# Moving the operands of TensorE's products to other byte offsets in SBUF: a conditioned decoder layer on one core

## The chip, the cores and the metric

The kernel runs on one core of one Trainium2 chip. The metric is the device time of one execution in microseconds (us), as the median of several runs. In the text, TensorE is PE (its weight loads PEld), VectorE is DVE, ScalarE is ACT, GpSimd is POOL and SyncE is SP, which issues most DMAs. SBUF is the on-chip memory of 128 partitions; a tile's "start" is its first byte within each partition. PSUM takes the results of TensorE.

## The reference

One layer of a decoder trunk for a batch of 1, 256 tokens, width 2048, in float32, followed by an RMS norm:

```python
mods = (silu(c) @ ada_w + ada_b).reshape(b, 9, d)
h = modulate(x, ffn1_norm, mods[:, 0], mods[:, 1])
x = x + 0.5 * mods[:, 2] * swiglu(h, ffn1_w_gate, ffn1_w_up, ffn1_w_down)   # 2048 -> 5632 -> 2048
h = modulate(x, mix_norm, mods[:, 3], mods[:, 4])
proj = h @ w_in                                       # columns for both mixers and the two gates
y_a = gated_delta_net(...) @ gdn_w_up                 # 8 heads of 128
y_b = sparse_attention(...) @ nsa_w_up                # 8 heads of 128
y = (m_a * y_a + m_b * y_b) @ w_out
x = x + mods[:, 5] * y
h = modulate(x, ffn2_norm, mods[:, 6], mods[:, 7])
x = x + 0.5 * mods[:, 8] * swiglu(h, ffn2_w_gate, ffn2_w_up, ffn2_w_down)
return rms_norm(x, final_norm)
```

Nearly all of the arithmetic lies in the products with the large weight matrices, which are read from HBM once.

## The kernel before, in words

Activations are kept transposed: a tile has 128 of the 2048 channels on its partitions and the 256 tokens along the free dimension. Weights arrive from HBM as tiles "raw" of 128 partitions by 8 slices of 128 columns (512 KB each), issued by SP.

To reach float32 accuracy with TensorE's fast float32r format, both operands of a product are split into a high and a low part. ACT copies raw to whi (line 186, or 357), which rounds it, and DVE writes the remainder raw - whi to wlo (line 187, or 358). Activations are pairs of 128 x 2 x 256: high part, then low part; they are called hpair (the input of a stage), apair (SwiGLU's result), xa (the unmodulated input of the second feed-forward stage), and oA, Vt, aT, Z, WT (the two mixers' outputs, which take over buffers of these names). The function product (line 192) issues, for each of its slices of 128 channels, two matmuls: line 196 with whi stationary and both halves of the pair moving (512 columns), then line 198 with wlo stationary and the high half moving (256 columns). This is called a pair of matmuls in the text; its weight loads are separate instructions on PEld, one for each matmul. The function block_rows (line 353) does the same in three matmuls of 256 columns for each slice (line 363); it serves the first stage's gate and up products and the first products of the stages that follow.

Order of the work: the start and the first feed-forward stage (functions start and ffn), the projections W_in with the two mixers beside them, the merge (line 1099: for each of 16 output tiles one weight tile of 16 slices; the first product takes slices 0 to 7 with the eight oA, the second slices 8 to 15 with Vt, aT, Z, WT, twice), W_out, the second feed-forward stage and the final norm. The reductions for the modulation (line 248, DVE) are spread between the products.

Memory: tiles come from pools, and a pool takes the next free stretch of SBUF when it is opened; within a pool, tiles stand in the order of their first use, each rounded up to 32 bytes. So a tile's start is the sum of all sizes before it. consts holds cf, vec (629 floats), cm (160 bytes), cr, cact and modc (9 x 16 floats); wp holds raw (8 buffers of 4096 bytes), whi and wlo (3 each); tp holds scratch tiles; nrm small tiles of the norms; hp the 16 hpair. The pool mp of the mixers is opened where the first stage's buffers were, so its tiles wait until these are done; its small tiles (gnw, na, ss, sk, m2 and so on, 4 to 480 bytes) stand between the large ones and set the starts of those behind them. A framework schedules the instructions of each engine from their dependences and the order of the code.

Of the kernel before, what the change touches and what calls it, by code (L numbers as in the profile page):

```python
# [18 lines left out]
F32 = mybir.dt.float32  # L19
F32R = mybir.dt.float32r  # L20
I32 = mybir.dt.int32
U8 = mybir.dt.uint8
# [5 lines left out]
P = 128  # L28
S = 256
D = 2048  # L30
KT = D // P
# [11 lines left out]
SIZES = ((4,), (4,), (4,), (4,))  # L43
LAG = 3
RES = 4
LT = 0
NE = 2
GK = 4
# [6 lines left out]
NB = 15  # L55
# [49 lines left out]
def trunk(tc, a, out, stage=99, dbg=None):  # L105
    nc = tc.nc
    ctx = ExitStack()
    with ctx:
        consts = ctx.enter_context(tc.tile_pool(name="consts", bufs=1))
# [13 lines left out]

        cf = consts.tile([P, C_END], F32, name="cf")
        nc.sync.dma_start(cf[:, :C_TRI], a["consts"][:, :C_TRI])
        vec = consts.tile([P, sum(n for _, n in VEC)], F32, name="vec")
        cm = consts.tile([P, 160], U8, name="cm")
        cr = consts.tile([P, 3, P], F32R, name="cr")
        ident = cf[:, C_ID:C_ID + P]
        ones = cf[:, C_ONE:C_ONE + P]  # L130
# [99 lines left out]
            nc.vector.tensor_sub(pair[:, 1], x, pair[:, 0])  # L230


        modc = consts.tile([P, 9, KT], F32, name="modc")
        ada_q = []

        def ada_cols(m, d, now=False):
# [47 lines left out]


        nrm = ctx.enter_context(tc.tile_pool(name="nrm", bufs=1))

        def square(ssq, d):
            if d == 0:
# [256 lines left out]
        def paces(*spans):  # L546
            todo = [(n, pace(total, n)) for total, n in spans]

            def f():
                while todo and todo[0][0] == 0:  # L550
                    todo.pop(0)
                if not todo:
                    return 0
                todo[0] = (todo[0][0] - 1, todo[0][1])
                return todo[0][1]()
            return f
# [29 lines left out]
        xpool.close()  # L586
        with ExitStack() as mx:
            mp = mx.enter_context(tc.tile_pool(name="mp", bufs=1))
            tk = paces((4, 31 - 2 * NE), (20, 20), (24, 36))

            beside = []
# [20 lines left out]
                return big(tag, BIG[tag], (P, 2, S), F32R)  # L612

            oA, oB = [None] * H, [None] * H
            gnw = mp.tile([P, 1], F32, name="gnw")
            nc.vector.tensor_scalar(gnw, V["gnw"], 0.5, None, op0=OP.mult)


# [1 line left out]
            both(win(0), sm)  # L620
            tok = mp.tile([P, 2, P], F32, name="tok")
            ge = mp.tile([P, 2, 2, 8], F32, name="ge")
            ngc = mp.tile([P, 2, 8], F32, name="ngc")
            na = mp.tile([P, 1], F32, name="na")
            beta = tok[:, :, 0:8]
            gtok = tok[:, :, 32:40]
            gate = tok[:, :, 64:88]
# [53 lines left out]
                return o  # L681

            def small(tag):
                return mp.tile([P, 4], F32, tag=tag, name=tag, bufs=2)

            def s3(t):
                return t.rearrange("p (a b) -> p a b", a=2)
# [17 lines left out]
            def gdn_group(h0, q, k, v):  # L705
# [3 lines left out]
                def tsl(p):  # L709
                    return slice(p * P, (p + 1) * P)  # L710

                ss = mp.tile([P, 2, 4], F32, tag="ss", name="ss", bufs=2)

                def flip(src):
                    pt = ptile((P, 4, P))
# [15 lines left out]
                pt = flip(q)  # L731
                squares(pt, ss[:, 1])
                nc.vector.tensor_scalar(ss, ss, 4 * EPS, None, op0=OP.add)
                rs = rsqrt(mp, ss, "rs")
                sk = small("sk")
                nc.vector.scalar_tensor_tensor(sk, rs[:, 0], 0.5 * RS, ss[:, 0], op0=OP.mult, op1=OP.mult)
                Cc = small("Cc")
# [136 lines left out]
                nc.vector.scalar_tensor_tensor(r2, rq, 1.0 / HD, rq, op0=OP.mult, op1=OP.mult)  # L874
                nc.vector.tensor_mul(so, so, r2)
                nc.vector.tensor_scalar(so, so, EPS, None, op0=OP.add)
                ro = rsqrt(mp, so, "ro")
                nc.vector.scalar_tensor_tensor(ro, ro, RS, rq, op0=OP.mult, op1=OP.mult)
                nc.vector.tensor_mul(o, o, ro.unsqueeze(2).to_broadcast([P, 4, P]))
                pt = ptile((P, 4, P))  # L880
# [18 lines left out]

            kcmp = mp.tile([P, 2 * NB], F32, name="kcmp")
            vcmp = mp.tile([16, 2, P], F32, name="vcmp")

            def compress():
                for b in range(2):
                    cat = mp.tile([P, 2, S], F32, tag="kk", name="cat", bufs=2)
                    for g in range(2):
                        both(win(W_KV + 2 * b + g, False), cat[:, g])
                        yield  # L910
                    G = mp.tile([P, 32, 32], F32, tag="G", name="G", bufs=1)
                    nc.gpsimd.memset(G[:, :, 2 * NB:], 0.0)
                    for g in range(2):
                        src = cat[:, g]
                        blocks = bass.AP(tensor=src.tensor, offset=src.offset, ap=[list(src.ap[0]), [1, 32], [16, NB]])
                        nc.vector.tensor_add(G[:, :, g * NB:(g + 1) * NB], blocks,
                                             V["pos"][:, 32 * b:32 * b + 32].unsqueeze(2).to_broadcast([P, 32, NB]))
                    ph = ftile()
                    for r in range(4):
                        (raw, _), = wload(a["cw1"][b][:, 8 * r:8 * r + 8], 8)  # L920
                        for j in range(8):
                            jj = 8 * r + j
                            q = slice(32 * (j % 4), 32 * (j % 4) + 32)
                            nc.tensor.matmul(ph[q, :P], G[:, jj], raw[:, j], start=(jj < 4), stop=(jj >= 28),
                                             skip_group_check=True)
                        yield
                    hs = mp.tile([P, P], F32, tag="hs", name="hs", bufs=1)
                    nc.scalar.activation(hs, ph[:, :P], AF.Copy)
                    pt = ftile()
                    nc.tensor.matmul(pt[:, :2 * NB], hs, cf[:, C_I32:C_I32 + 2 * NB], start=True, stop=True)  # L930
                    hid = mp.tile([P, 2 * NB], F32, tag="hid", name="hid", bufs=1)
                    nc.scalar.activation(hid, pt[:, :2 * NB], AF.Identity, bias=V["b1"][:, b:b + 1])
                    th = tmpc()[:, :2 * NB]
                    nc.scalar.activation(th, hid, AF.Tanh, scale=0.5)
                    hT2 = tmpc()[:, :2 * NB]
                    nc.vector.scalar_tensor_tensor(hT2, th, 1.0, hid, op0=OP.add, op1=OP.mult)
                    w2 = V["w2"][:, b * P:(b + 1) * P]
                    pc = ftile()
                    if b == 0:
                        nc.tensor.matmul(pc[:, :2 * NB], w2, hT2, start=True, stop=True)  # L940
                        nc.scalar.activation(kcmp, pc[:, :2 * NB], AF.Copy, scale=0.5)
                    else:
                        for g in range(2):
# [42 lines left out]
            def compressed(g, qs, gg):  # L986

                psc = ptile((P, 2, 4, 16))
                for qt in range(2):
                    for r in range(4):  # L990
                        nc.tensor.matmul(psc[:, qt, r, :NB], qs[r][:, qt * P:(qt + 1) * P],
                                         kcmp[:, g * NB:(g + 1) * NB], start=True, stop=True)
                sc = mp.tile([P, 2, 4, NB], F32, tag="sc", name="sc", bufs=1)
                cmask = cf[:, C_CMP:C_CMP + 32].rearrange("p (a b) -> p a b", a=2)
                for qt in range(2):
                    nc.vector.tensor_add(sc[:, qt], psc[:, qt, :, :NB],
                                         cmask[:, qt, :NB].unsqueeze(1).to_broadcast([P, 4, NB]))
                cmx = mp.tile([P, 8], F32, tag="cmx", name="cmx", bufs=2)
                scf = sc.rearrange("p a b c -> p (a b) c")
                nc.vector.tensor_reduce(cmx, scf, axis=AX.X, op=OP.max)  # L1000
                nc.vector.tensor_scalar(cmx, cmx, NEG / 10, None, op0=OP.max)
                nc.vector.tensor_sub(scf, scf, cmx.unsqueeze(2).to_broadcast([P, 8, NB]))
                nc.scalar.activation(sc, sc, AF.Exp, scale=SCALE)
                den = mp.tile([P, 8], F32, tag="den", name="den", bufs=2)
                nc.vector.tensor_reduce(den, scf, axis=AX.X, op=OP.add)
                nc.vector.tensor_scalar(den, den, 0.5, None, op0=OP.max)
                nc.vector.reciprocal(den, den)
                d3 = den.rearrange("p (q r) -> p q r", q=2)
                nc.vector.tensor_mul(d3, d3, gg[:, :, :, 0])
                nc.vector.tensor_mul(scf, scf, den.unsqueeze(2).to_broadcast([P, 8, NB]))  # L1010
                return sc

            def attend(g, kk, vt, qs):
# [3 lines left out]
                def soft(r, qt):  # L1017
# [4 lines left out]
                    for b in range(2):  # L1022
# [1 line left out]
                                         start=(b == 0), stop=False, skip_group_check=True)  # L1024
                    nc.tensor.matmul(ps[:, :, n - P:n], ident_r, cr[:, 2].unsqueeze(1).to_broadcast([P, 2, P]),
                                     start=False, stop=True, skip_group_check=True)
                    m2 = mp.tile([P, 2], F32, tag="m2", name="m2", bufs=4)
                    nc.vector.tensor_reduce(m2, ps[:, :, :n], axis=AX.X, op=OP.max)
                    nc.vector.tensor_scalar(m2, m2, -SCALE, None, op0=OP.mult)
                    p_ = pr[r, qt] = big(*PR[(2 * r + qt) % 3], (P, 2, S))  # L1030
                    dn = mp.tile([P, 2], F32, tag="dn", name="dn", bufs=4)
                    for b in range(2):
                        nc.scalar.activation(p_[:, b, :n], ps[:, b, :n], AF.Exp, bias=m2[:, b:b + 1],
                                             scale=SCALE, accum_out=dn[:, b:b + 1])
# [189 lines left out]
```

## Time and profile before

| | us |
|---|---|
| median of 3 runs (lowest, highest) | 2324.71 (2324.65, 2325.98) |
| the profiled execution | 2323.47 |
| its span, first to last instruction | 2321.6 |
| busy: PE, PEld, DVE, ACT | 2272.6, 2028.3, 1776.4, 1133.3 |

The mean granted TensorE clock of the profiled execution was 0.997 of full speed. 564 MB were read from HBM, 245 GB/s over the span. How to read the views: the page lists the busy time of each engine and the chain of work that ended last, followed back from the end; the groups put together instructions of one line, operation and shape, with their count, total busy time and mean duration, and after the bar the idle time ahead of them and what ended it; the timeline lists instructions by start time. Matmuls are pipelined, so a matmul's duration in the profile is longer than the distance from its start to the next one's.

### The profile page before, as it was taken

To read this page: it belongs to the slowest core of one execution; us is meant where nothing else is said; L and a number is where in the kernel's file an instruction comes from. 1 tells how busy PE (TensorE), PEld (TensorE's weight loads), DVE (VectorE), ACT (ScalarE), POOL (GpSimd) and SP (SyncE) were. 2 spreads that over 40 slices of the span, in tenths; PEclk is the share of its full clock that TensorE was granted. 3 is DMA by queue.
4 is the path that set the end of the run, shared out by engine and by line. 5 is a ranking of instruction groups with operands and counts; after the bars stand their busy time and mean duration, and the time that the engine had idled before them with its cause. 6 is when DMAs were issued, how large, how long until landed. Compare 5 with 4: busy or idle time off the path is not lost.

```text
span 2321.6 us, 39012 instructions
## 1 busy us (share of the span) xinstructions
PE 2272.6 (98%) x15130; PEld 2028.3 (87%) x15130; DVE 1776.4 (77%) x2896; ACT 1133.3 (49%) x1788; POOL 1.5 (0%) x8
## 2 busy tenths in 40 slices
PE   6999999999999999999999999999999999999997
PEld 5999988888888978887888888889888888888886
DVE  6799888878887787789997887787666666555565
ACT  3544554434444565554555445556444444344453
POOL 0000000000000000000000000000000000000000
PEclk9999999999999999999999999999999999999999
DMA  8999689888987646548677897665777777665663
GB/s 317 318 331 332 200 280 335 296 297 322 337 308 248 213 141 199 185 156 268 238 270 244 312 318 262 221 229 183 244 244 243 238 235 216 192 198 190 183 189 104
DMA packets 174493, 571.00 MB, mean 246 GB/s; under 512 B 17890, under 2 KB 18146, under 8 KB 174308
## 3 DMA queue, kind: packets, MB, share of 16 engines
q1 hardware_dynamic: 173584, 566.09, 73.0%
q8 instruction: 118, 1.93, 0.3%
q10 hardware_dynamic: 724, 2.43, 0.3%
q14 instruction: 67, 0.55, 0.1%
HBM read 564.25 MB, written 4.19 MB: 245 GB/s over the span
## 4 chain that ended last, share of the span: by engine, by line
PE 90%; DVE 6%; ACT 2%; DMA 1%; issue 1%; DVEq 0%; SPq 0%; ACTq 0%
PE mm L196 48%; PE mm L198 26%; PE mm L363 9%; PE c L363 2%; DVE adaraw L248 1%; DVE wlo L187 1%; DVE wlo L358 1%; DMA raw<-in_win_dram 1%; PE c L433 1%; DMA cf<-in_consts_dram 0%; PE c L1023 0%; ACT whi L186 0%; ACT junk L723 0%; PE c L800 0%; DMA raw<-in_w1gu_dram 0%
## 5 line engine op out<-in xcount | busy, mean ns | idle before, releaser
L196 PE MATMUL mm<-hpair,whi 128*128 128x512 f32 x3536 | 1237.7, 392 | 2.0 <-ACT t L218 2.0
L187 DVE TENSOR_TENSOR wlo<-raw,whi 128x1024 fp32r<-128x1024 f32 (+1 forms) x666 | 796.8, 1196 | 419.3 <-ACT whi L186 417.2
L186 ACT ACTIVATE whi<-raw 128x1024 fp32r<-128x1024 f32 (+1 forms) x666 | 691.9, 1039 | 755.1 <-PE mm L196 381.7
L198 PE MATMUL mm<-hpair,wlo 128*128 128x256 f32 x3536 | 1002.7, 284 | 2.6 <-DVE wlo L187 2.6
L196 PEld LDWEIGHTS mm<-hpair,whi 128*128 128x128 f32 x3536 | 664.4, 188 | 140.6 <-ACT t L218 2.5
L198 PEld LDWEIGHTS mm<-hpair,wlo 128*128 128x128 f32 x3536 | 668.7, 189 | 6.5 <-DVE wlo L187 4.0
L196 PE MATMUL mm<-apair,whi 128*128 128x512 f32 x1408 | 488.3, 390 | 0.0
L198 PE MATMUL mm<-apair,wlo 128*128 128x256 f32 x1408 | 397.1, 282 | 0.0
L196 PEld LDWEIGHTS mm<-apair,whi 128*128 128x128 f32 x1408 | 264.4, 188 | 55.4
L363 PE MATMUL mm<-hpair,whi 128*128 128x256 f32 x1472 | 260.7, 280 | 5.7 <-ACT whi L357 5.7
L198 PEld LDWEIGHTS mm<-apair,wlo 128*128 128x128 f32 x1408 | 266.1, 189 | 0.0
L363 PEld LDWEIGHTS mm<-hpair,whi 128*128 128x128 f32 x1472 | 225.9, 189 | 6.0 <-ACT whi L357 6.0
L363 PE MATMUL mm<-hpair,wlo 128*128 128x256 f32 x736 | 207.2, 282 | 3.1 <-DVE wlo L358 3.0
L248 DVE CUSTOM_DVE_ANT_0 adaraw<-adaraw,cact,vec 128x1024 f32<-128x1024 f32 x144 | 183.6, 1275 | 13.2 <-DMA adaraw<-in_ada_w_dram 13.2
L248 DVE CUSTOM_DVE_ANT_0 adaraw<-adaraw,cact,part 128x1024 f32<-128x1024 f32 x144 | 183.8, 1277 | 0.0
L357 ACT ACTIVATE whi<-raw 128x1024 fp32r<-128x1024 f32 x112 | 118.3, 1058 | 113.6 <-PE mm L363 44.3
L358 DVE TENSOR_TENSOR wlo<-raw,whi 128x1024 fp32r<-128x1024 f32 x112 | 136.1, 1220 | 34.0 <-ACT whi L357 33.5
L363 PEld LDWEIGHTS mm<-hpair,wlo 128*128 128x128 f32 x736 | 139.2, 189 | 4.2 <-DVE wlo L358 3.8
L222 ACT ACTIVATE t<-mm 128x256 f32<-128x256 f32 x237 | 86.5, 367 | 2.6 <-PE mm L198 2.6
L225 DVE TENSOR_TENSOR t<-mm,t 128x256 f32<-128x256 f32 x193 | 80.5, 417 | 2.7 <-ACT t L222 2.5
L530 DVE SCALAR_TENSOR_TENSOR xT<-mm,g,xT 128x256 f32<-128x256 f32 x128 | 61.5, 481 | 7.1 <-PE mm L198 5.4
L515 ACT ACTIVATE t<-t 128x256 f32<-128x256 f32 x63 | 25.9, 411 | 50.1 <-DVE t L225 50.1
(359 smaller groups left out, 1502.3 us busy)
## 6 DMA issues: line engine op xcount, KB each, us to landing
adaraw<-in_ada_w_dram SPq DMA_DIRECT2D x288, 512.0 KB, 5.7
raw<-in_w2gu_dram SPq DMA_DIRECT2D x180, 512.0 KB, 4.6
raw<-in_w1gu_dram SPq DMA_DIRECT2D x176, 512.0 KB, 5.9
raw<-in_win_dram SPq DMA_DIRECT2D x158, 512.0 KB, 5.2
raw<-in_w1d_dram SPq DMA_DIRECT2D x64, 512.0 KB, 5.1
raw<-in_w2d_dram SPq DMA_DIRECT2D x64, 512.0 KB, 4.1
raw<-in_wup_dram SPq DMA_DIRECT2D x32, 512.0 KB, 4.9
raw<-in_wout_dram SPq DMA_DIRECT2D x32, 512.0 KB, 4.7
```

The costliest lines, as they stand in the source:

```text
L186: nc.scalar.activation(hi[:, :n], raw[:, :n], AF.Copy)
L187: behind(nc.vector.tensor_sub(lo[:, :n], raw[:, :n], hi[:, :n]))
L196: nc.tensor.matmul(ps[:, :], hi, pairs[k][:, :, :].rearrange("p a b -> p (a b)"), start=(k == 0), stop=False, skip_group_check=True)
L198: nc.tensor.matmul(ps[:, S:2 * S], lo, pairs[k][:, 0, :], start=False, stop=(k == n - 1), skip_group_check=True)
L222: nc.scalar.activation(t, ps[:, S:2 * S], AF.Copy)
L225: nc.vector.tensor_add(o, ps[:, :S], t)
L248: nc.vector.tensor_tensor_reduce(out=raw, in0=raw, in1=cact[:, hf * HC:(hf + 1) * HC], scale=1.0, scalar=part[0], op0=OP.mult, op1=OP.add, ...
L357: nc.scalar.activation(hi, raw, AF.Copy)
L358: behind(nc.vector.tensor_sub(lo, raw, hi))
L363: nc.tensor.matmul(ps[:, w], l[:, w, k], h[:, r], start=(first and w == k == x == 0), stop=(last and k == kb - 1 and x == 2), skip_group_c ...
L515: nc.scalar.activation(s, g, AF.Silu, bias=bg)
L530: nc.vector.scalar_tensor_tensor(xT[:, d], pd[:, j * S:(j + 1) * S], g05[:, d:d + 1], xT[:, d], op0=OP.mult, op1=OP.add)
```

## The change

No instruction is added to the computation or taken from it, and no size of an operation changes. The change moves tiles to other starts:

- consts: vec is rounded up to 640 floats, cm to 256 bytes, modc to 10 x 16 floats, so that all that follows starts at multiples of 128.
- nrm gets a tile "pad" of 40 floats that nothing uses; it shifts hp and everything behind it.
- The mixers' small tiles move from mp to a pool of their own, ms, which is opened behind mp.

```diff
+PAD = 40
...
-        vec = consts.tile([P, sum(n for _, n in VEC)], F32, name="vec")
-        cm = consts.tile([P, 160], U8, name="cm")
+        nv = sum(n for _, n in VEC)
+        vec = consts.tile([P, -(-nv // 32) * 32], F32, name="vec")[:, :nv]
+        cm = consts.tile([P, 256], U8, name="cm")[:, :160]
...
-        modc = consts.tile([P, 9, KT], F32, name="modc")
+        modc = consts.tile([P, 10, KT], F32, name="modc")[:, :9]
...
         nrm = ctx.enter_context(tc.tile_pool(name="nrm", bufs=1))
+        nrm.tile([P, PAD], F32, name="pad")
...
             mp = mx.enter_context(tc.tile_pool(name="mp", bufs=1))
+            ms = mx.enter_context(tc.tile_pool(name="ms", bufs=1))
...
-            gnw = mp.tile([P, 1], F32, name="gnw")
+            gnw = ms.tile([P, 1], F32, name="gnw")
...
-            na = mp.tile([P, 1], F32, name="na")
+            na = ms.tile([P, 1], F32, name="na")
```

and so on for ngc, ss, the tiles of small(), rsqrt's, kcmp, hid, sc, cmx, den, m2 and dn. The starts in the two built programs, in bytes from the partition's beginning (of the first buffer; all buffers of a tile have the same remainder modulo 128):

| tile | role in a product | start before | modulo 128 | start after | modulo 128 |
|---|---|---|---|---|---|
| raw | what whi and wlo are split from | 35392 | 64 | 35584 | 0 |
| whi | stationary | 68160 | 64 | 68352 | 0 |
| wlo | stationary | 80448 | 64 | 80640 | 0 |
| hpair | moving | 102496 | 96 | 102848 | 64 |
| apair, xa | moving | 151648 | 96 | 152000 | 64 |
| Vt, aT, Z, WT | moving | 166752, 170848, 148832, 175968 | 96 | 166464, 170560, 149056, 175680 | 64 |
| oA | moving | 197408 | 32 | 196672 | 64 |

Slices of whi and wlo lie 512 bytes apart, the two halves of a pair 1024, so they have the same remainders.

The schedule changes at a few places, because the tiles of ms lie in memory that nothing used before them. On ACT, near the program's start, before (cact is the activated conditioning vector, t the squares of the input, cr constants for the mixers, rb the inverse norms spread over the partitions):

```order
L148 ACTIVATE cact<-c 128x512
L431 ACTIVATE t<-xT 128x256 x15
L156 ACTIVATE cr<-cf 128x128
L483 ACTIVATE rb<-c 128x256
L323 ACTIVATE hpair<-t,modc 128x256 x2
L357 ACTIVATE whi<-raw 128x1024
```

The same place after; na is the exponential of one parameter vector of the delta-rule mixer:

```order
L151 ACTIVATE cact<-c 128x512
L435 ACTIVATE t<-xT 128x256 x15
L159 ACTIVATE cr<-cf 128x128
L645 ACT_TABLE_LOAD
L645 ACTIVATE na<-vec 8x1
L487 ACTIVATE rb<-c 128x256
L327 ACTIVATE hpair<-t,modc 128x256 x2
L361 ACTIVATE whi<-raw 128x1024
```

The exponential and a load of its table moved here from the mixers' beginning. The second place on ACT is the end of the function start, where the first SwiGLU activations (t from gu) and the splits of their results (apair) begin; before:

```order
L323 ACTIVATE hpair<-t,modc 128x256
L357 ACTIVATE whi<-raw 128x1024 x4
L470 ACTIVATE t<-gu 128x256
L229 ACTIVATE apair<-t 128x256
L357 ACTIVATE whi<-raw 128x1024
L470 ACTIVATE t<-gu 128x256
```

and after:

```order
L327 ACTIVATE hpair<-t,modc 128x256
L361 ACTIVATE whi<-raw 128x1024 x4
L474 ACT_TABLE_LOAD
L474 ACTIVATE t<-gu 128x256
L361 ACTIVATE whi<-raw 128x1024
L232 ACTIVATE apair<-t 128x256
```

A second table load stands here, and the split of the result stands behind the next copy of weights. In all, ACT has seven table loads after and five before. On DVE, the one-column operation for gnw moves from the mixers' beginning to the program's start; TensorE's order changes in one place, where two small transposes stand two matmuls later.

More of the change, by code (lines that the diff above doesn't have):

```diff
@@ L622, in trunk @@
             ge = mp.tile([P, 2, 2, 8], F32, name="ge")
-            ngc = mp.tile([P, 2, 8], F32, name="ngc")
-            na = mp.tile([P, 1], F32, name="na")
+            ngc = ms.tile([P, 2, 8], F32, name="ngc")
+            na = ms.tile([P, 1], F32, name="na")
             beta = tok[:, :, 0:8]
@@ L683, in small @@
             def small(tag):
-                return mp.tile([P, 4], F32, tag=tag, name=tag, bufs=2)
+                return ms.tile([P, 4], F32, tag=tag, name=tag, bufs=2)
             def s3(t):
@@ L710, in tsl @@
                     return slice(p * P, (p + 1) * P)
-                ss = mp.tile([P, 2, 4], F32, tag="ss", name="ss", bufs=2)
+                ss = ms.tile([P, 2, 4], F32, tag="ss", name="ss", bufs=2)
                 def flip(src):
@@ L733, in gdn_group @@
                 nc.vector.tensor_scalar(ss, ss, 4 * EPS, None, op0=OP.add)
-                rs = rsqrt(mp, ss, "rs")
+                rs = rsqrt(ms, ss, "rs")
                 sk = small("sk")
@@ L876, in gdn_group @@
                 nc.vector.tensor_scalar(so, so, EPS, None, op0=OP.add)
-                ro = rsqrt(mp, so, "ro")
+                ro = rsqrt(ms, so, "ro")
                 nc.vector.scalar_tensor_tensor(ro, ro, RS, rq, op0=OP.mult, op1=OP.mult)
@@ L898, in gdn_out @@
                     split(oA[h], sg)
-            kcmp = mp.tile([P, 2 * NB], F32, name="kcmp")
+            kcmp = ms.tile([P, 2 * NB], F32, name="kcmp")
             vcmp = mp.tile([16, 2, P], F32, name="vcmp")
@@ L930, in compress @@
                     nc.tensor.matmul(pt[:, :2 * NB], hs, cf[:, C_I32:C_I32 + 2 * NB], start=True, stop=True)
-                    hid = mp.tile([P, 2 * NB], F32, tag="hid", name="hid", bufs=1)
+                    hid = ms.tile([P, 2 * NB], F32, tag="hid", name="hid", bufs=1)
                     nc.scalar.activation(hid, pt[:, :2 * NB], AF.Identity, bias=V["b1"][:, b:b + 1])
@@ L992, in compressed @@
                                          kcmp[:, g * NB:(g + 1) * NB], start=True, stop=True)
-                sc = mp.tile([P, 2, 4, NB], F32, tag="sc", name="sc", bufs=1)
+                sc = ms.tile([P, 2, 4, NB], F32, tag="sc", name="sc", bufs=1)
                 cmask = cf[:, C_CMP:C_CMP + 32].rearrange("p (a b) -> p a b", a=2)
@@ L997, in compressed @@
                                          cmask[:, qt, :NB].unsqueeze(1).to_broadcast([P, 4, NB]))
-                cmx = mp.tile([P, 8], F32, tag="cmx", name="cmx", bufs=2)
+                cmx = ms.tile([P, 8], F32, tag="cmx", name="cmx", bufs=2)
                 scf = sc.rearrange("p a b c -> p (a b) c")
@@ L1003, in compressed @@
                 nc.scalar.activation(sc, sc, AF.Exp, scale=SCALE)
-                den = mp.tile([P, 8], F32, tag="den", name="den", bufs=2)
+                den = ms.tile([P, 8], F32, tag="den", name="den", bufs=2)
                 nc.vector.tensor_reduce(den, scf, axis=AX.X, op=OP.add)
@@ L1026, in soft @@
                                      start=False, stop=True, skip_group_check=True)
-                    m2 = mp.tile([P, 2], F32, tag="m2", name="m2", bufs=4)
+                    m2 = ms.tile([P, 2], F32, tag="m2", name="m2", bufs=4)
                     nc.vector.tensor_reduce(m2, ps[:, :, :n], axis=AX.X, op=OP.max)
@@ L1030, in soft @@
                     p_ = pr[r, qt] = big(*PR[(2 * r + qt) % 3], (P, 2, S))
-                    dn = mp.tile([P, 2], F32, tag="dn", name="dn", bufs=4)
+                    dn = ms.tile([P, 2], F32, tag="dn", name="dn", bufs=4)
                     for b in range(2):
```

## The prediction

> **What bounds the kernel now.** I read the page first, then the chain of work that ended last, then the groups of instructions with shapes kept apart, then the timeline of TensorE in a few places, and last the windows of 100 us. The page says which engine it is:
>
> ```profile
> span 2321.6 us, 39012 instructions
> PE 2272.6 (98%) x15130; PEld 2028.3 (87%) x15130; DVE 1776.4 (77%) x2896; ACT 1133.3 (49%) x1788; POOL 1.5 (0%) x8
> ...
> PE 90%; DVE 6%; ACT 2%; DMA 1%; issue 1%; DVEq 0%; SPq 0%; ACTq 0%
> ```
>
> TensorE's matmuls are 90% of the chain that sets the end. The groups say which matmuls (the columns are line, engine, operation, what it reads, shape and count, then total busy time and mean ns of one):
>
> ```profile
> L196 PE MATMUL mm<-hpair,whi 128*128 128x512 f32 x3536 | 1237.7, 392 | 2.0 <-ACT t L218 2.0
> L196 PE MATMUL mm<-apair,whi 128*128 128x512 f32 x1408 | 488.3, 390 | 0.0
> L363 PE MATMUL mm<-hpair,whi 128*128 128x256 f32 x1472 | 260.7, 280 | 5.7 <-ACT whi L357 5.7
> L363 PE MATMUL mm<-hpair,wlo 128*128 128x256 f32 x736 | 207.2, 282 | 3.1 <-DVE wlo L358 3.0
> L196 PE MATMUL mm<-oA,whi 128*128 128x512 f32 x128 | 45.8, 396 | 0.0
> L363 PE MATMUL c<-hpair,whi 128*128 128x256 f32 x256 | 45.1, 279 | 0.0
> L363 PE MATMUL c<-hpair,wlo 128*128 128x256 f32 x128 | 35.9, 281 | 0.6 <-DVE wlo L358 0.6
> L196 PE MATMUL mm<-Vt,whi 128*128 128x512 f32 x32 | 12.5, 392 | 0.0
> L196 PE MATMUL mm<-aT,whi 128*128 128x512 f32 x32 | 12.5, 391 | 0.0
> L196 PE MATMUL mm<-Z,whi 128*128 128x512 f32 x32 | 12.5, 390 | 0.0
> L196 PE MATMUL mm<-WT,whi 128*128 128x512 f32 x32 | 12.5, 390 | 0.0
> ```
>
> Each L196 matmul (512 columns) is followed by one at L198 (256 columns) with the low part of the same weights. That makes 3536 + 1408 + 128 + 4 x 32 = 5200 pairs, and 1472 + 736 + 256 + 128 = 2592 single matmuls of L363. The idle times in the last column are a few us in all, so these matmuls wait for nobody: what counts is how far apart two starts are. The means (392, 284 ns) overlap from one matmul to the next and are no price; the price is the distance of starts in the timeline (start us, then duration). A steady stretch, first a pair, and the 30th pair behind it, and in between the weight load that belongs to the next pair:
>
> ```profile
> 1899.85 0.39 PE L196 MATMUL mm<-hpair,whi 128*128 128x512 f32 x1
> 1900.07 0.28 PE L198 MATMUL mm<-hpair,wlo 128*128 128x256 f32 x1
> ...
> 1910.25 0.39 PE L196 MATMUL mm<-hpair,whi 128*128 128x512 f32 x1
> ```
>
> ```profile
> 1900.08 0.19 PEld L196 LDWEIGHTS mm<-hpair,whi 128*128 128x128 f32 x1
> ```
>
> A pair takes 10.40 us / 30 = 346.7 ns, of which the 512 columns take about 228 and the 256 about 118. The load of the next weights starts 0.01 us after the matmul that it runs beside: two reads of SBUF by TensorE, one of the stationary and one of the moving operand, run at once. The single matmuls of L363:
>
> ```profile
> 265.21 0.28 PE L363 MATMUL mm<-hpair,wlo 128*128 128x256 f32 x1
> ...
> 266.26 0.28 PE L363 MATMUL mm<-hpair,wlo 128*128 128x256 f32 x1
> ```
>
> Between these two rows lie nine starts, 1.05 us / 9 = 116.7 ns each. So 5200 x 346.7 ns + 2592 x 116.7 ns = 1803 + 302 = 2105 us of the span's 2321.6 are paid in these two prices, and a nanosecond on a pair is 5.2 us.
>
> **Does the start of an operand matter at all?** The kernel holds an experiment of its own. In the merge stage one product runs over 16 slices of one kind of weights, first against eight oA tiles, then against eight Vt, aT, Z and WT tiles. By the buffers' starts (the table in the section on the change) the weights begin 64 bytes behind a multiple of 128, oA at 32 behind one, the other tiles at 96. Engine, shapes, weights and neighbours are the same:
>
> ```profile
> 1304.99 0.39 PE L196 MATMUL mm<-oA,whi 128*128 128x512 f32 x1
> ...
> 1305.34 0.39 PE L196 MATMUL mm<-oA,whi 128*128 128x512 f32 x1
> ...
> 1305.69 0.40 PE L196 MATMUL mm<-oA,whi 128*128 128x512 f32 x1
> ...
> 1306.05 0.39 PE L196 MATMUL mm<-oA,whi 128*128 128x512 f32 x1
> ...
> 1307.81 0.39 PE L196 MATMUL mm<-Vt,whi 128*128 128x512 f32 x1
> ...
> 1310.59 0.39 PE L196 MATMUL mm<-hpair,whi 128*128 128x512 f32 x1
> ```
>
> The eight oA pairs take 1307.81 - 1304.99 = 2.82 us, 352.5 ns each, the eight others 2.78 us, 347.5 ns each. Within oA the pairs alternate: 0.35 us (1305.34 to 1305.69), then 0.36 (1305.69 to 1306.05). The group rows say the same: L196's mean is 396 ns for oA and 390 to 392 for all others. So where operands lie moves a pair by 5 ns on average and by more than 10 at its worst.
>
> [...]
>
> **The change part by part.** *The starts* (consts rounded to multiples of 128, the pad, the pool ms). All 5200 pairs and all 2592 singles get weights at a multiple of 128 and moving operands 64 behind one. No row of the trace has that combination: the moving operand lies 32 behind the weights in nearly all pairs, and 96 behind them in oA's. Bounds for a pair: from above, the worst oA pair, 0.36 us. From below, rows in which only one of the two reads works hard:
>
> ```profile
> 1129.32 1.86 PE L991 MATMUL c<-kcmp,q 128*128 128x15 f32 x16
> 1131.03 1.11 PE L1023 MATMUL c<-kk,qr 128*128 128x256 f32 x4
> ...
> 1139.59 0.60 PE L1058 MATMUL c<-pT,vt 128*128 128x256 f32 x2
> 1140.02 0.38 PE L1060 MATMUL c<-pT,vt 128*128 128x128 f32 x2
> ```
>
> L991's matmuls move 15 columns, so the weight loads set their distance: 1.71 us / 16 = 107 ns. L1058's float32 matmuls move half as fast (256 columns in 0.43 / 2 = 215 ns, with a load beside them); 512 columns of a product could hardly go below that. A pair bounded so costs 215 + 107 = 322 ns, a single 107. The excess of today's prices over these is 24.7 ns a pair and 9.7 a single: 128 + 25 = 153 us that contention of the two reads could explain at most, and an unknown part of it is a fixed cost of changing weights.
>
> Which value? Two distances are known, 96 (352.5 ns) and 32 (346.7 ns, the steady rows). The step between them, 5.8 ns, is the only measured size of the effect; I take one such step more, downwards, for the new distance: half a line of 128 apart, with both operands on multiples of 64, looks the kindest to two readers. That is a choice, not a row. 5200 x 5.8 ns = 30 us, and for the singles the same per column (three of 256 columns are a pair's 768): 2592 / 3 x 5.8 ns = 5 us. Together -35 us.
>
> *The other engines* must feed a TensorE that is 1.7% faster. The tightest windows (window, length, busy us of PE, PEld, DVE, ACT, POOL, clock, DMA share, GB/s):
>
> ```profile
> 300.00:400.00 100.00, 100.00 (x578) 88.65 (x578) 86.27 (x125) 49.46 (x73) 0.00 (x0) 1.00 0.91 318
> 1100.00:1200.00 100.00, 97.84 (x588) 84.74 (x588) 93.28 (x226) 51.97 (x118) 0.00 (x0) 1.00 0.76 261
> ```
>
> DMA would go from 0.91 to 0.93, DVE from 93 to 95: not binding at this size. At 7% (322 ns) they would be: 0.98.
>
> *The instructions that move.* The pool ms lies in memory that no earlier pool used, so the Exp of na no longer waits for the first stage's buffers and moves to the front of ACT, and brings a table load with it; a second load brings Silu's table back before L470. Durations and places:
>
> ```profile
> 4.79 1.28 ACT L148 ACT_TABLE_LOAD   x1 [4.79 <-DMA cf<-in_consts_dram]
> 20.86 0.29 ACT L156 ACTIVATE cr<-cf 128x128 fp32r<-128x128 f32 x1
> 35.74 0.38 ACT L483 ACTIVATE rb<-c 128x256 f32<-128x256 f32 x1 [14.59 <-PE c L309]
> ...
> 237.06 1.06 ACT L357 ACTIVATE whi<-raw 128x1024 fp32r<-128x1024 f32 x1 [1.69 <-PE mm L363]
> 239.75 0.42 ACT L229 ACTIVATE apair<-t 128x256 fp32r<-128x256 f32 x1 [1.33 <-DVE t L471]
> ```
>
> The first load falls into the 14.59 us in which ACT waits for the sums. The second stands ahead of L470 near 238 us, where ACT waits 1.69 us before its copy and 1.33 us behind, with three buffers of split weights ahead of TensorE: nothing, or 1.3 us if the cover fails. DVE's gnw (one column) goes the same way. The mixer's three loads stay three. Sum of the moves: 0, at most 2.6 us.
>
> The profiled execution took 2323.5 us, 1.9 around its span; the sum there is 2323.5 - 35 = 2288.5, and the median of the runs lies 1.2 higher: 2290.
>
> **The rivals.** *Nothing changes.* The 0.35 us pairs of oA are as short as the steady 346.7: two different distances reach the same value, which looks like a floor. Then the excess is the fixed cost of changing weights, the oA rows show only that one can do worse, and the time is 2324.7 plus at most 2.6. Against it: 228 ns where the float32 rows need 215.
>
> *Slower: the new distance is a bad one.* If 64 collides as oA's does, all pairs cost 352.5 ns: (5200 - 128) x 5.8 ns + 5 us = +34, 2359; if every pair is a 0.36, 13.3 x 5.2 = +69, 2394. It decides from 347.6 ns a pair on (0.9 x 5.2 = 4.7 us). For it: the alternation inside oA shows that neither the start modulo 128 nor the distance alone decides, so a uniform distance may be uniformly bad. Against it: only 128 of 5200 pairs show it now.
>
> *Much faster: most of the excess goes.* Half of 153 us gives 2248, all of it 2172, where DMA at 0.98 and DVE in the mixer would take over first. For it: both 228 and 118 lie well above their bounds. [...]
>
> That the change does not do what it says is no rival: the starts of the built program are those of the table.
>
> **How the numbers follow.** One step faster (2290): 0.42. Much faster: 0.18. Nothing: 0.20. Slower: 0.20. A measurement of this kernel can tell about 0.2% from no change, 4.6 us. So faster 0.60, same 0.20, slower 0.20. For the range I leave out half of the much faster case (0.09) and half of the slower one (0.10): from 2225, about two thirds of the excess, to 2345, about 4 ns a pair more. The likeliest case alone, half a step to two steps, is 2255 to 2307.
>
> **What would show it.** Right: in the steady stretch of the second feed-forward stage thirty pairs take about 10.2 us instead of 10.40, the L196 mean of oA is that of the others, and the alternation in oA is gone. Nothing: 10.40 again, with oA alone repaired. Slower: pairs of 0.35 and 0.36 in turn in all stages. The moves are wrong if TensorE's first L363 matmul starts later than now or if a gap appears near 240 us. The forecast fails if pairs stay within 1 ns of 346.7 or rise; its size fails if DMA or DVE shows new waits ahead of the splits (L186, L187) while pairs got shorter.

## The result and the profile after

The changed kernel takes 2354.95 us (median of 4 runs, 2352.9 to 2357.16), the kernel before beside it 2324.68 us (4 runs, 2323.08 to 2325.98): a ratio of 1.0132, 95% interval 1.0118 to 1.0146. It is slower by 30 us, where 2290 was forecast. The profiled execution took 2357.16 us; from its page the span, the engines and the chain that ended last:

```profile
span 2355.4 us, 39014 instructions
PE 2303.3 (98%) x15130; PEld 2024.0 (86%) x15130; DVE 1778.7 (76%) x2896; ACT 1136.4 (48%) x1790; POOL 1.5 (0%) x8
...
PE 91%; DVE 5%; ACT 2%; DMA 1%; issue 1%; DVEq 0%; ACTq 0%; SPq 0%
```

The span grew by 33.8 us (2355.4 - 2321.6). PE's busy time grew by 30.7, DVE's and ACT's by 2 to 3, and the chain has the same owners: the loss lies inside TensorE's own work. The groups (columns as in the prediction) say in which matmuls:

```profile
L199 PE MATMUL mm<-hpair,whi 128*128 128x512 f32 x3536 | 1261.1, 399 | 4.3 <-ACT t L221 4.3
L199 PE MATMUL mm<-apair,whi 128*128 128x512 f32 x1408 | 497.7, 397 | 0.0
L199 PE MATMUL mm<-oA,whi 128*128 128x512 f32 x128 | 45.9, 396 | 0.0
L199 PE MATMUL mm<-Vt,whi 128*128 128x512 f32 x32 | 12.6, 395 | 0.0
L201 PE MATMUL mm<-apair,wlo 128*128 128x256 f32 x1408 | 395.6, 281 | 0.0
L367 PE MATMUL mm<-hpair,whi 128*128 128x256 f32 x1472 | 256.9, 279 | 5.7 <-ACT whi L361 5.7
```

The counts are what they were and the idle times are still a few us. The mean of apair's 512 columns rose from 390 to 397 ns, hpair's from 392 to 399, and oA, which stood out before, now has the same 396 as its neighbours. The steady stretch of the second feed-forward stage, a pair and the 30th pair behind it:

```profile
1924.94 0.40 PE L199 MATMUL mm<-hpair,whi 128*128 128x512 f32 x1
1925.17 0.28 PE L201 MATMUL mm<-hpair,wlo 128*128 128x256 f32 x1
...
1935.54 0.40 PE L199 MATMUL mm<-hpair,whi 128*128 128x512 f32 x1
```

10.60 us / 30 = 353.3 ns a pair, where it was 346.7: 6.6 ns more, times 5200 pairs 34 us, the whole of the span's 33.8. Start to start, the 512 columns went from 228.3 to 235.0 ns and the 256 columns stayed at 118.3. In the merge the eight oA pairs and the eight others now cost nearly the same, 2.82 and 2.83 us:

```profile
1321.78 0.40 PE L199 MATMUL mm<-oA,whi 128*128 128x512 f32 x1
...
1324.60 0.39 PE L199 MATMUL mm<-Vt,whi 128*128 128x512 f32 x1
...
1327.43 0.39 PE L199 MATMUL mm<-hpair,whi 128*128 128x512 f32 x1
```

So oA was not made good; all the others were made as bad as oA. The moved instructions behave as the prediction had it. ACT's timeline with the first of the two added table loads (start, duration, in brackets the wait ahead):

```profile
20.93 0.29 ACT L159 ACTIVATE cr<-cf 128x128 fp32r<-128x128 f32 x1
21.24 1.28 ACT L645 ACT_TABLE_LOAD   x1
22.53 0.20 ACT L645 ACTIVATE na<-vec 8x1 f32<-8x1 f32 x1
...
35.81 0.39 ACT L487 ACTIVATE rb<-c 128x256 f32<-128x256 f32 x1 [13.08 <-PE c L313]
```

The load falls into ACT's wait, which shrinks from 14.59 to 13.08 us, and rb comes 0.07 us later than before. The line's own view of L199 puts hpair's first pair at 295.7 us (the first number behind the durations), as that of L196 before had 295.8:

```profile
L196 PE MATMUL mm<-hpair,whi x3536: 388/390/628, 295.8 to 2184.1; 128*128 128x512 f32 x197
```

```profile
L199 PE MATMUL mm<-hpair,whi x3536: 388/397/628, 295.7 to 2215.4; 128*128 128x512 f32 x197
```

Up to 296 us, where only single matmuls run, nothing was lost or won. From there on, where nearly all of the pairs run, the lag grows to 31.3 us at the last hpair pair (2215.4 - 2184.1).

### The profile page after: what moved, and what is told of

Read it like the earlier page. It is cut to its first block, busy times and chain, and to the rows that moved or that the text cites. A ratio compares the mean times of both kernels' runs of the same rounds, so it can differ in the third digit from the quotient of the medians.

```text
span 2355.4 us, 39014 instructions
## 1 busy us (share of the span) xinstructions
PE 2303.3 (98%) x15130; PEld 2024.0 (86%) x15130; DVE 1778.7 (76%) x2896; ACT 1136.4 (48%) x1790; POOL 1.5 (0%) x8
## 4 chain that ended last, share of the span: by engine, by line
PE 91%; DVE 5%; ACT 2%; DMA 1%; issue 1%; DVEq 0%; ACTq 0%; SPq 0%
PE mm L199 49%; PE mm L201 25%; PE mm L367 11%; PE c L367 1%; DMA raw<-in_win_dram 1%; DVE adaraw L251 1%; DVE wlo L190 1%; PE c L437 1%; DVE wlo L362 1%; PE c L1028 0%; ACT junk L728 0%; ACT whi L189 0%; PE c L805 0%; PE c L1063 0%; PE c L150 0%
## 5 line engine op out<-in xcount | busy, mean ns | idle before, releaser
L199 PE MATMUL mm<-hpair,whi 128*128 128x512 f32 x3536 | 1261.1, 399 | 4.3 <-ACT t L221 4.3
L199 PEld LDWEIGHTS mm<-hpair,whi 128*128 128x128 f32 x3536 | 666.0, 188 | 165.9 <-ACT t L221 4.8
L199 PE MATMUL mm<-apair,whi 128*128 128x512 f32 x1408 | 497.7, 397 | 0.0
L199 PEld LDWEIGHTS mm<-apair,whi 128*128 128x128 f32 x1408 | 264.7, 188 | 65.5
L361 ACT ACTIVATE whi<-raw 128x1024 fp32r<-128x1024 f32 x112 | 118.3, 1059 | 115.4 <-PE mm L367 39.5
```

What stands on the lines that cost most here:

```text
L199: nc.tensor.matmul(ps[:, :], hi, pairs[k][:, :, :].rearrange("p a b -> p (a b)"), start=(k == 0), stop=False, skip_group_check=True)
L361: nc.scalar.activation(hi, raw, AF.Copy)
```

## The experiments

The theory after the result: the price of a pair is set by the distance between the start of the moving operand and that of the weights, and the change took nearly all pairs from a distance of 32 to one of 192 (modulo 256; 64 modulo 128). The mixers' outputs, 256 of the 5200 pairs, lie elsewhere: by the table of starts oA went from 224 to 64, Vt, aT, Z and WT from 32 to 64. Rivals: weights at multiples of 128 are bad by themselves; the moving operand's own start decides; the moved instructions cost it. In what follows "distance" is the moving operand's start minus the weights', modulo 256, and prices are start-to-start means over a steady stretch.

**The price without the layer.** A kernel that leaves the layer out and only runs pairs (and triples of 256 columns, as L363 does) over a grid of starts in steps of 16 bytes, with no other engine and no DMA beside it:

```diff
+        steps = range(0, 128, 16)
...
+        for w in steps:
+            for m in steps:
+                for k in range(32):
+                    j = k % 4
+                    x = M[m][:, 512 * j:512 * j + 512]
+                    nc.tensor.matmul(ps[:, :], W["hi", w][:, P * j:P * j + P], x, start=(k == 0), stop=False,
+                                     skip_group_check=True)
+                    nc.tensor.matmul(ps[:, S:], W["lo", w][:, P * j:P * j + P], x[:, :S], start=False,
+                                     stop=(k == 31), skip_group_check=True)
```

> This kernel leaves out the whole layer and only repeats the products' pair of matmuls (512 columns against the high weights, then 256 against the low ones) for 64 combinations: weights and moving operands each at 0, 16, ... 112 bytes behind a multiple of 1024; then L363's form of three matmuls of 256 columns for 16 combinations in steps of 32. If the distance modulo 128 decides, the pair costs the same along each diagonal of the table: about 347 ns where the moving operand lies 32 behind the weights, 352 to 353 where it lies 64 or 96 behind them. If the moving operand's own start decides, the cost is the same along each of its columns: 347 at 96, 353 at 64, about 352 at 32, whatever the weights. If the weights' own start decides, it is the same along each row: 347 at 64, 353 at 0. If a step of 16 matters in itself, the odd multiples of 16 stand out from their neighbours.

It took 826.6 us. The prices of pairs are the layer's own: 346.7 ns with weights at 64 and the moving operand at 96 (before), 353.3 with 0 and 64 (after). So neither HBM traffic nor ACT's and DVE's reads make them; two operands of TensorE do. With weights at multiples of 32 the prices are equal along the diagonals of the grid, which is what a distance means. But weights at 0 with 96 cost 350.0 and weights at 64 with 32 cost 346.7, though both are 96 apart modulo 128, which points to a period longer than 128. Weights at odd multiples of 16 have other prices, the lowest 343.3. Of the series with weights at 64 and the moving operand at 32, a pair and the 20th behind it (6.93 us / 20):

```profile
392.35 0.39 PE L134 MATMUL ps<-mv,hi 128*128 128x512 f32 x1
...
399.28 0.39 PE L134 MATMUL ps<-mv,hi 128*128 128x512 f32 x1
```

This distance is -32, that is 224 modulo 256, at which oA's pairs cost 352.5 ns in the layer before. So the distance alone does not fix the price there.

**One half of the change at a time.** Only the size of the pad (and of modc) changes against the changed kernel, which sets other distances:

```diff
-PAD = 40
+PAD = 16
```

The weights stay at 0 modulo 128 and hpair and apair come to 96, a distance of 96.

> Weights at a multiple of 128 as in the change, all moving operands at 96 behind one as before (the pad is 16 floats instead of 40). By the distance (96, as oA's before): about 352.5 ns a pair, 2350 to 2358 us. By the moving operand's own start: 347 ns a pair, 2320 to 2328 us. By the weights' own start: 353 ns a pair, 2352 to 2358 us.

2347.81 us (2347.44 to 2350.06), ratio 1.0096 (1.0081 to 1.0111). A pair takes 350.1 ns, the steady single matmuls 120.0. The mixers' outputs lie at 224 here, where oA lay before, in the same stage of the same layer; yet the first eight oA pairs take 2.78 us, 347.5 ns each, and do not alternate (the group's mean is 392 ns against 396):

```profile
1320.20 0.40 PE L199 MATMUL mm<-oA,whi 128*128 128x512 f32 x1
...
1322.98 0.39 PE L199 MATMUL mm<-Vt,whi 128*128 128x512 f32 x1
```

So 224 has a cheap price in the layer too. The next kernel:

```diff
-PAD = 40
+PAD = 24
...
-        modc = consts.tile([P, 10, KT], F32, name="modc")[:, :9]
+        modc = consts.tile([P, 11, KT], F32, name="modc")[:, :9]
```

Weights and moving operands are both at 64 modulo 128. The expectation calls this the distance 0, counting modulo 128; modulo 256 it is 128 for hpair and apair.

> Weights at 64 behind a multiple of 128 as before, all moving operands at 64 as in the change, so that the distance is 0. By the moving operand's own start: 353 ns a pair, 2350 to 2358 us. By the weights' own start: 347 ns a pair, 2320 to 2328 us. The distance 0 has no row so far; by the distance any price other than these two may come, between 340 and 361 ns.

2351.05 us (2349.29 to 2351.98), 1.0105 (1.0088 to 1.0122); a pair 351.1, singles 118.7. Each half alone costs time too, so neither half is the harmful one.

```diff
-PAD = 40
-        nrm.tile([P, PAD], F32, name="pad")
...
-        vec = consts.tile([P, -(-nv // 32) * 32], F32, name="vec")[:, :nv]
+        vec = consts.tile([P, nv], F32, name="vec")
```

(and cm and modc likewise as they were; the pool ms stays)

> The mixers' small tiles in a pool of their own as in the change, with its moved instructions and two more table loads, but consts not rounded and no pad: weights at 64, all moving operands (oA too) at 96. If the starts are the whole loss: 346.7 ns a pair, oA's pairs as the others, 2321 to 2327 us (oA's repair is worth 0.7 us). If the moved instructions carry the loss: 2350 us or more.

2327.31 us (2325.23 to 2329.47), 1.0003 (0.9994 to 1.0012); a pair 346.7. All moved instructions, both table loads included, cost nothing that can be measured, and with them that rival is gone.

**The period.** The same grid without the layer, with the moving operand's start run through 1024 bytes in steps of 32 against weights at 0, and over shorter stretches against weights at 64, 256 and 16:

```diff
+        for w, ms in ((0, range(0, 1024, 32)), (64, range(64, 576, 32)), (256, range(256, 768, 64)),
+                      (16, range(16, 528, 32)), (0, range(16, 512, 64))):
+            for m in ms:
+                pairs(w, m)
```

> This kernel too leaves out the layer and only repeats pairs and triples of matmuls, all reading one moving tile, one high and one low weight tile, with starts chosen by the slice: weights at 0, moving operands 0 to 992 bytes further in steps of 32; then weights at 64, 256 and 16 with distances over 512 bytes. If the distance modulo 128 decides, the table repeats every 128 bytes and distance 192 costs what 64 does. If the distance modulo 512 decides (the stages' distances are 32 before, 192 after, 96 and 128 in the two half changes, 224 for oA before), the table gives 347, 353, 350, 351 and 352 ns at these five, it repeats after 512 but not after 128, and it is the same for weights at 0, 64 and 256.

It took 1113.6 us. At distances in steps of 32 the prices of pairs repeat every 256 bytes, neither 128 nor 512, and are the same for weights at 0, 64 and 256, but for the distance 0, where series at 346.7 and at 353 stand side by side. Of TensorE's timeline the first and the 20th pair behind it at distances of 32, 192 and 288:

```profile
39.89 0.39 PE L135 MATMUL ps<-mv,hi 128*128 128x512 f32 x1
...
46.82 0.39 PE L135 MATMUL ps<-mv,hi 128*128 128x512 f32 x1
...
95.84 0.40 PE L135 MATMUL ps<-mv,hi 128*128 128x512 f32 x1
...
102.91 0.40 PE L135 MATMUL ps<-mv,hi 128*128 128x512 f32 x1
...
129.71 0.39 PE L135 MATMUL ps<-mv,hi 128*128 128x512 f32 x1
...
136.64 0.39 PE L135 MATMUL ps<-mv,hi 128*128 128x512 f32 x1
```

6.93 us for 20 pairs at 32, 7.07 at 192, 6.93 again at 288 = 256 + 32. That the period is not 128 shows at 96, where every series takes 350.0 ns and at 224 none does, and in the triples, which take 353.4 ns at 32 and 356.1 at 160 with weights at 0. The whole table, ns a pair, as this grid gives it and, behind "or", where a series of another grid in steps of 16 or 8 bytes gave something else:

| distance modulo 256 | 0 | 32 | 64 | 96 | 128 | 160 | 192 | 224 |
|---|---|---|---|---|---|---|---|---|
| weights at multiples of 32 | 346.7 or 353 | 346.7 | 353.3 or 348.9 | 350.0 | 351.0 | 346.7 | 353.3 | 353.7 or 346.7 |
| weights 16 behind one | 348.2 or 346.7 | 353.3 | 346.7 | 350.1 | 350.2 | 350 or 346.7 | 351 or 353.3 | 343.3 |

In the upper row the distances 32, 96, 128, 160 and 192 have one price, within 0.3 ns, in every grid that runs them; 0, 64 and 224 have two. What decides between the two is open: the first grid ran its three series at 224 at 346.7, this one all six at 353.7. (At odd multiples of 16 against weights at 0 two prices occur as well: 353.3 and 350.0 for two series at 80.) The layer's kernels so far sit in the upper row: 32 before (oA at 224), 192 after, 96 and 128 in the two halves. The prediction had counted oA's 224 and the other operands' 32 as 96 and 32 modulo 128.

**Three kernels to break this table.** First the change without its pad: the weights stay at multiples of 128, and the distance is back at 32.

```diff
-PAD = 40
...
-        nrm.tile([P, PAD], F32, name="pad")
```

> The change with its rounded consts and its pool ms, but without the pad: weights at a multiple of 128 (256 modulo 512), hpair and apair at 288 modulo 512, so that the distance is 32 as before. If the distance decides: 346.7 ns a pair and 116 to 119 a single, 2321 to 2332 us. If weights at a multiple of 128 are bad in themselves: 2340 us or more.

2327.4 us (2323.15 to 2332.2), 1.0012 (1.0003 to 1.0022); a pair 346.7. Weights at multiples of 128 are not bad in themselves: the same weights' starts modulo 128, 40 floats less in front of the moving operands, and all but some 0.1% of the loss is gone.

Then two distances that no kernel had tried, a low price and a high one:

```diff
-PAD = 40
+PAD = 32
```

This is the distance 160.

> The change with a pad of 32 floats: hpair, apair and xa lie 160 behind the weights (modulo 256), the mixers' outputs 32. By the distance modulo 256 (the grid has 346.7 ns a pair and 356.2 a triple at 160): 864 triples cost about 6 ns more than before, 2325 to 2334 us. If every distance other than 32 costs a pair 3 ns or more: 2340 us or more.

2330.02 us (2327.53 to 2335.16), 1.0020 (1.0011 to 1.0029); a pair 346.7, as the table says.

```diff
-PAD = 40
+PAD = 48
...
-        cm = consts.tile([P, 256], U8, name="cm")[:, :160]
+        cm = consts.tile([P, 160], U8, name="cm")
```

This is the distance 224.

> The change with a pad of 48 floats and cm not rounded: hpair, apair and xa lie 224 behind the weights modulo 256, the mixers' outputs 96. By the distance modulo 256 (353.7 ns a pair, 350 for the mixers' outputs, 355 a triple): 2324.5 + 4944 x 7.0 + 256 x 3.3 ns + 864 x 5 ns, about 2364, 2356 to 2370 us, the slowest of all. By the distance modulo 128 (224 is then 96): 350 a pair and 360 a triple as in the run with the weights alone moved, 2345 to 2353 us.

2357.62 us (2356.26 to 2359.5), 1.0136 (1.0119 to 1.0153). That is what period 256 gave (2356 to 2370) and not what period 128 gave (2345 to 2353). The forecast used the dearer of the two prices at 224, and the layer took that one here, 352.1 ns a pair on average for hpair and 353.3 for apair. Its groups, with oA now at another distance than hpair and apair:

```profile
L199 PE MATMUL mm<-hpair,whi 128*128 128x512 f32 x3536 | 1256.8, 398 | 4.3 <-ACT t L221 4.3
L199 PE MATMUL mm<-apair,whi 128*128 128x512 f32 x1408 | 497.7, 397 | 0.0
L199 PE MATMUL mm<-oA,whi 128*128 128x512 f32 x128 | 45.5, 393 | 0.0
```

Now oA (96) is the cheap one with 393 ns, and hpair and apair (224) have the 397 to 398 that oA had before at the same distance. Its pairs also alternate, as oA's did:

```profile
1919.80 0.39 PE L199 MATMUL mm<-hpair,whi 128*128 128x512 f32 x1
...
1920.14 0.40 PE L199 MATMUL mm<-hpair,whi 128*128 128x512 f32 x1
...
1920.51 0.39 PE L199 MATMUL mm<-hpair,whi 128*128 128x512 f32 x1
...
1920.85 0.40 PE L199 MATMUL mm<-hpair,whi 128*128 128x512 f32 x1
```

0.34 us, 0.37, 0.34. So the alternation is not bound to oA's neighbours or place. Nor does it come with the distance 224 every time: with the weights alone moved, oA lay at 224 and ran at 347.5 ns without it.

**Finer steps.** The kernel without the layer once more, in steps of 8 bytes:

```diff
+        for w in (0, 8, 16, 24):
+            for m in range(0, 256, 8):
+                pairs(w, w + m, 24)
```

> Again only pairs and triples of matmuls, the layer left out: weights at 0, 8, 16 and 24 bytes, distances from 0 to 248 in steps of 8. If both reads work in units of 16 bytes, weights at 8 or 24 cost what those at 0 or 16 cost give or take 1 ns, and nothing comes below the 343.3 ns a pair and 340 ns a triple of the grids in steps of 16. If the unit is finer, new prices between 322 and 343 ns may appear at multiples of 8.

It took 1300.29 us. No pair falls below 343.3 to 343.5 ns, at weights 16 behind a multiple of 32 and distance 224. Weights at 8 or 24 cost 346 to 360. So an unused gain of 3.4 ns a pair exists (5200 x 3.4 = 18 us), but only with both operands at odd multiples of 16, and the triples there cost 360 (3 x 120) against 353.4 at before's distance, some 2.2 ns on each of 2592 singles, 6 us back. No run tested it in the layer: the tiles of the table of starts all begin at multiples of 32 bytes, so the operands would have to be parts of larger tiles, and to keep one distance for all buffers each has to grow by 256 bytes; for the 6 buffers of weights and the 16 hpair alone that is 5.6 KB.

**What the price is made of.** Is it the weight load reading beside the matmul all the while? A kernel without the layer again, with series of equal matmuls whose weight loads take 128, 64 or 32 columns:

```diff
+        def single(m, cols, n, reps=32):
+            for k in range(reps):
+                j = k % 4
+                nc.tensor.matmul(ps[:cols, :n], W["hi" if k % 2 else "lo"][:, P * j:P * j + cols], x_(m, j, 0, n),
+                                 start=(k == 0), stop=(k == reps - 1), skip_group_check=True)
...
+        for n in (512, 256):
+            for cols in (128, 64, 32):
+                for m in range(0, 256, 32):
+                    single(m, cols, n)
```

> The layer is left out: series of equal matmuls, 512 or 256 moving columns, each with a weight load of its own of 128, 64 or 32 columns, at distances 0 to 224 in steps of 32. If the reads of the next weights and of the moving operand collide, what a 512-column matmul takes beyond 215 ns shrinks with the load (12 to 20 ns at 128 columns, about half of it at 64, a quarter at 32), and so does its spread over the distances. If it is a fixed cost of changing weights, the excess stays at 12 ns or more at 64 and 32 columns. If the moving operand's own start were slow, the spread over the distances would stay.

It took 306.56 us. The groups of its weight loads and of the 512-column matmuls (low and high part in turn; busy us, mean ns, idle us):

```profile
L150 PEld LDWEIGHTS ps<-mv,lo 128*128 128x128 f32 x256 | 48.2, 188 | 5.8
L150 PEld LDWEIGHTS ps<-mv,lo 128*64 128x64 f32 x256 | 34.4, 134 | 12.2
L150 PEld LDWEIGHTS ps<-mv,hi 128*32 128x32 f32 x256 | 27.7, 108 | 16.9
...
L150 PE MATMUL ps<-mv,hi 128*128 128x512 f32 x128 | 50.5, 394 | 0.0
L150 PE MATMUL ps<-mv,hi 128*32 128x512 f32 x128 | 50.4, 394 | 0.0
```

The load shrinks from 188 to 108 ns and the matmul does not notice: 394 ns both times. Start to start over 20 matmuls at distance 32, first with 128 columns loaded, then with 32:

```profile
35.55 0.39 PE L150 MATMUL ps<-mv,lo 128*128 128x512 f32 x1
...
40.21 0.39 PE L150 MATMUL ps<-mv,lo 128*128 128x512 f32 x1
...
154.03 0.39 PE L150 MATMUL ps<-mv,lo 128*32 128x512 f32 x1
...
158.69 0.39 PE L150 MATMUL ps<-mv,lo 128*32 128x512 f32 x1
```

4.66 us / 20 = 233 ns in both. Over all eight distances 512 columns cost 226.7 to 234.3 ns with 128 columns loaded, 226.7 to 231.7 with 64 and 230.2 to 233.3 with 32; 256 columns cost 113.3 to 120.0 with 128 and 113.3 to 117.8 with 32. The theory that the two reads collide as long as the load lasts falls: a quarter of the columns should have left a quarter of the excess over 215 ns (the estimate from the float32 row of L1058), and it left nearly all (18 ns of 18 at distance 32). Loading less only narrows the spread over the distances (7.6, 5.0 and 3.1 ns). What happens inside at a change of weights, why the period is 256 bytes, and what puts a series into the cheap or the dear of two prices, stays open.

## Why the prediction was wrong

**What held.** TensorE's matmuls are still nine tenths of the chain; 5200 pairs at 5.2 us a nanosecond carry the result; the moved instructions cost nothing (the kernel with them alone: 1.0003); DMA and DVE became no bound (1% and 5% of the chain after, 1% and 6% before). The count of 2592 singles leaves out the 96 that move xa (2688 in all), which at the 1.9 ns forecast for each is 0.2 us.

**The step that failed** is the value taken for the new distance: "I take one such step more, downwards, for the new distance: half a line of 128 apart, with both operands on multiples of 64, looks the kindest to two readers. That is a choice, not a row." The step was to be -5.8 ns a pair; it was +6.6. The two measured distances were read modulo 128, as 96 and 32, and a line was drawn through them to a third that no row had. Modulo 256 they are 224 and 32, the new one is 192, and the table between them goes up and down with no slope to follow. Besides, the 352.5 of 224 is one of two prices there. The rows held the caution that was needed: 352.5 was known to be possible, and the low end, 215 + 107 ns, was the author's estimate from two small float32 products (L1058, L991); the lowest series of equal matmuls with 128 columns loaded took 226.7 ns for 512 columns and 113.3 for 256. The floor that the rival "nothing changes" named is there: before's 346.7 is the lowest price that a distance in steps of 32 gave with weights at multiples of 32.

**The rival that came true** is "the new distance is a bad one", priced at 352.5 ns a pair and 2359 us; measured were 353.3 and 2354.95. Its reason for was right as well: "neither the start modulo 128 nor the distance alone decides, so a uniform distance may be uniformly bad". That its number came so close is luck: 352.5 is a mean over oA's pairs at 224, which alternate between some 346 and 360 ns, while at 192 nearly every pair takes 353 to 354, and the pairs of 0.35 and 0.36 that were to show it did not appear. Its reason against, that only 128 of 5200 pairs showed it, was no evidence, since those 128 were the only ones at another distance.

**The singles** were to gain 1.9 ns each. In the steady parts of their stage (starts less than 135 ns apart, 60 to 296 us) they take 115.2 ns on average where it was 116.7, but not evenly: 113.4 between 100 and 200 us, and 117.8 between 240 and 280 us, more than before. So the size of the gain is near the forecast by luck, and no time came of it. The windows of the stage (length; PE, PEld, DVE, ACT, POOL; clock, DMA share, GB/s), before and after:

```profile
60.00:296.00 236.00, 234.75 (x1997) 233.63 (x1997) 208.72 (x297) 114.15 (x155) 0.00 (x0) 1.00 0.85 293
```

```profile
60.00:296.00 236.00, 233.85 (x1999) 231.38 (x1998) 208.69 (x297) 115.47 (x156) 0.00 (x0) 1.00 0.85 293
```

1997 and 1999 matmuls in 236 us are 118.2 and 118.1 ns each, whatever the steady parts say. What 1.5 ns on 1958 matmuls wins, 3.0 us, goes in longer distances: 20 starts before lie 135 ns or more behind the one ahead, 36 after, and beyond 118 ns each they add up to 3.0 and 5.9 us. Many of them begin at a first use of wlo, and the weight loads' waits for it grew (us in total, times, longest), before and after:

```profile
PEld mm L363 <- DVE wlo L358: 1.0, 2, 0.7
PEld c L363 <- DVE wlo L358: 0.8, 1, 0.8
```

```profile
PEld c L367 <- DVE wlo L362: 1.8, 2, 1.0
PEld mm L367 <- DVE wlo L362: 1.2, 2, 0.8
```

All five kernels whose singles take up to 117.7 ns in steady parts have 1992 to 1999 matmuls in this window, those at 118.3 to 120.0 have 1955 to 1977 (236 / 1955 = 120.7). The author's estimate from these counts is a floor near 118 ns set by the supply of split weights, with DMA at 0.85 the nearest candidate behind it; no run tested it.

**The sum over all kernels.** Changes of price against before, times 5200 and 2592, beside the change of span (us; singles as the mean of the steady parts, 116.7 before):

| kernel | distance | pair, ns | single, ns | sum | span |
|---|---|---|---|---|---|
| after | 192 | 353.3 | 115.2 | +34 - 4 | +33.8 |
| weights only | 96 | 350.1 | 120.0 | +18 + 9 | +24.3 |
| moving only | 128 | 351.1 | 118.7 | +23 + 5 | +28.6 |
| moves only | 32 | 346.7 | 117.7 | 0 + 3 | +2.2 |
| no pad | 32 | 346.7 | 116.8 | 0 + 0 | +5.2 |
| distance 160 | 160 | 346.7 | 117.4 | 0 + 2 | +7.9 |
| distance 224 | 224 | 352.1 to 353.3 | 118.3 | +28 to 34, + 4 | +34.3 |

The pairs order the kernels; the rest stays within about 6 us, the scatter of single executions included. The distance is that of hpair and apair; the 256 pairs of the mixers' outputs are counted at the same price, which is off by less than 1 us in each row. No kernel beats the one before: no distance in steps of 32, with weights at multiples of 32, gave a pair a lower price than its distance does.

## What to carry to other kernels

When operands' places are changed in a kernel that TensorE bounds, measure the price of the exact sequence of matmuls over a grid of starts first: a kernel of a millisecond without any of the layer gave the layer's prices of pairs within 0.3 ns at the distances that have one price (32, 96, 128, 160, 192), and both of the prices at 224. Rounding the starts to 128 brought nothing by itself (1.0012 without the pad), and two known points of a price that depends on addresses are no slope; until its period is known, the honest forecast for a third point is the spread of the known ones. Here 7 ns in 350 were worth 1.3% of the program, and the layout before already stood at the best of them.

## What the runs showed of the hardware

- In these runs the start-to-start price of float32r matmuls that each have their own weights went with the distance between the two operands' starts, with a period of 256 bytes (20 pairs in 6.93 us at 32, 7.07 at 192, 6.93 at 288), and with whether the weights start at an even or odd multiple of 16: 343.3 to 353.7 ns for 512 + 256 columns with distances in steps of 32. The 512-column matmul took the difference between before and after (228.3 or 235.0 ns), the 256-column one none (118.3).
- Weights at multiples of 32: distances 32 and 160 cost 346.7 ns a pair, 96 350.0, 128 351.0, 192 353.3, in the grids and in the layer's kernels alike.
- Again with weights at multiples of 32, at the distances 0, 64 and 224 a series runs at one of two prices. 0 has 346.7 or 353, 64 353.3 or (in one series) 348.9, 224 346.7 without alternation or 353.7 with it (229 and 240 ns in turn for the 512 columns). What decides is open.
- Prices of pairs and triples often lie at 340.0, 343.3, 346.7, 350.0, 353.3 or 360.0, some 3.3 ns or twice that apart, but not all do: 348.2, 351.0 and 355.1 occur too.
- A weight load of 128, 64 or 32 columns lasts 188, 134 or 108 ns in the profile; the 512-column matmuls beside it last 394, 392 and 394.
